# Reordering the opening of a two-layer trunk kernel and spreading its modulation chunks

## The chip, the cores and the metric

The kernel runs on one core of a Trainium2 chip. The metric is device time in microseconds for one whole execution; the median of the runs counts. The core has a matrix engine (PE, with its weight loads shown apart as PEld), a vector engine (DVE), a scalar engine (ACT), a general engine (POOL) and a sequencer (SP) that in this kernel issues every DMA. Each engine works through its own instructions in a fixed order. SP's order matters in the same way: a DMA that must wait for a buffer holds up every DMA behind it.

## The reference

The reference is a backbone of two layers over 1024 latent tokens and 256 context tokens of width 1024. Each layer has two halves, each begun by an RMS norm and a modulation, whose shift, scale and gate come from one product of a small vector with `w_ada`:

```python
def modulation(cond, w_ada, b_ada):
    m = jax.nn.silu(cond) @ w_ada + b_ada
    return [t[..., None, :] for t in jnp.split(m, 6, axis=-1)]
...
sh1, sc1, g1, sh2, sc2, g2 = modulation(c, w_ada[i], b_ada[i])
csh1, csc1, cg1, csh2, csc2, cg2 = modulation(c_ctx, w_ada[i], b_ada[i])
h = modulate(rms_norm(x, norm1_g[i]), sh1, sc1)
hc = modulate(rms_norm(ctx, norm1_g[i]), csh1, csc1)
a_z, bq, bk, bv, cq, ck, cv = split_proj(h @ w_in[i])
...
x = x + g1 * (jnp.concatenate([out_a, out_b, out_c], axis=-1) @ w_out[i])
x = x + g2 * conv_ffn(modulate(rms_norm(x, norm2_g[i]), sh2, sc2), w_up[i], conv_w[i], conv_b[i], w_down[i])
```

The three outputs are a gated MLP over chunks of 128 positions, a windowed attention and a differential attention. All data is float32.

## The kernel before

Tokens are cut into ten tiles of 128: 0 to 7 are latent, 8 and 9 are context. `w_ada` of a layer is [1024, 6144]; the kernel takes its columns in twelve chunks of 512. Chunks 0 and 1 are the shift of the first half, 2 and 3 its scale, 4 and 5 its gate; 6 to 11 are shift, scale and gate of the second half. A chunk is 2 MB, read in four transfers of 512 KB. `mod_chunk` multiplies it on PE with the two vectors, padded to 32 columns, in four 32-column strips of the array at once (line 144), copies the sums out of PSUM (line 146), transposes them (line 149), adds over the strips (line 151) and adds the bias (line 153). `mod_scale` (line 192) then makes the factor of the norm from chunks 2 and 3.

A token tile is loaded and transposed by `load_x` (line 326 is its load, lines 335 to 339 the transposes and copies, line 340 a store of the transposed tile), normalised and modulated by `norm_tile` (lines 208 to 216 the norm, 220 and 222 the modulation, 223 and 109 the split into a high and a low half). The result `h` is what the input projection multiplies.

`inproj` multiplies tiles by one block of 512 columns of `w_in` (blocks 3, 2, 1, 0): 24 matmuls a tile (line 132). The block's weights come in four units of 512 KB (`wunit`, line 113 the load), each split by ACT (line 115) and DVE (line 109) into halves. The raw loads share a ring of three buffers, tag `raw` in pool `wr`; three units of split weights lie in `ws`, the fourth in `wx`. What comes out is copied to a buffer `zs` (line 412, four of them) and goes through norm and rotation (lines 352 to 373), or, in block 0, through the gated MLP (lines 434 to 459), and is stored (lines 391, 463).

Layer 0 takes the tiles in two groups, `al` = (8, 9, 0, 1, 2) and `be` = (3 to 7). In program order: chunks 2, 3, 0, 1; the small tables (`setup`, `setup2`); norms of `al`; blocks 3, 2 of `al`; norms of `be`; blocks 1, 0 of `al` with the context attention; blocks 3, 2, 1 of `be`; chunks 4 to 7; block 0 of `be`; chunks 8 to 11. For chunks 4 to 11 the transfers use the same `raw` ring as the weights. Attention of the latent tiles and the output projection (line 130 with `oT`) follow.

The order on each engine is not the program's. A planner simulates the program and issues, on each engine, what it thinks is ready, earlier code first; so a change in one place moves instructions on all engines for a long way.

Of the kernel before, what the change touches and what calls it, by code (L numbers as in the profile page):

```python
# [52 lines left out]
def trunk(ctx: ExitStack, tc: tile.TileContext, a: dict):  # L53
# [35 lines left out]
    wb = {"zs": 4, "sq": 3, "kn": 3, "st": 2}  # L89
# [45 lines left out]
    def mod_chunk(L, ch, mkps, mkpt, ev, mkraw):  # L135
        ps = mkps()
        for c in range(2):
            for kth in range(2):
                raw = mkraw()
                c0 = ch * 512 + c * 256  # L140
                sp.dma_start(out=raw, in_=a["w_ada"][L, kth * 512:kth * 512 + 512, c0:c0 + 256]
                             .rearrange("(k p) c -> p k c", p=P))
                for j in range(4):
                    pe.matmul(ps[32 * j:32 * j + 32, c * 256:c * 256 + 256], cpad[:, 4 * kth + j, :], raw[:, j, :],
                              start=(kth == 0), stop=(kth == 1))
        dve.tensor_copy(ev, ps)
        pt = mkpt()
# [48 lines left out]
    def norm_tile(L, which, src, s, hi, lo, mkps, mkbig, f=None, ss=None, eng=pool, add='a'):  # L196
# [19 lines left out]
        dve.tensor_tensor(out=f, in0=src, in1=bc[:, 0:P].unsqueeze(1).to_broadcast([P, KT, P]), op=ALU.mult)  # L216
        for k in range(KT):
# [51 lines left out]
    def setup2(ini, L, mkp):  # L269
# [6 lines left out]
        for nm, d in (("c", 32), ("b", 64)):  # L276
            base = ini.tile([P, 2, NT // P, d], F32, tag=f"base{nm}", name="tbase")
            sp.dma_start(out=base, in_=a[f"k_rope_{nm}"].rearrange("(i p) c d -> p c i d", p=P))
            for w in "kq":
# [12 lines left out]
                for c in range(2):  # L292
# [928 lines left out]
```

## Time and profile before

| what | value |
|---|---|
| median of 3 runs | 3370.29 us (3367.59 to 3371.93) |
| the profiled execution | 3366.29 us, its span 3364.5 us |
| PE busy | 3160.1 us, 94% of the span |
| DVE, ACT busy | 2473.2 us (74%), 1669.9 us (50%) |
| mean granted PE clock | 0.971 |
| DMA | 499.50 MB, mean 148 GB/s |

The window view gives, for a stretch of time, busy microseconds of PE, PEld, DVE, ACT and POOL (instruction counts in brackets), the granted PE clock, the busy share of the 16 DMA engines and GB/s. The timeline gives start, duration, engine, line, operation, output and inputs, and in square brackets the idle time before it and what ended it. SPq rows are DMA issues, not transfers. The group view gives busy time and mean nanoseconds of one, and after the bar the idle time before, with what ended it. The matrix engine is busy nearly throughout, so what can be gained there is idle time and time at a reduced clock.

### The profile page before, as it was taken

How to read it: one execution, taken by the hardware profiler on the slowest of the kernel's cores; microseconds unless marked ns; L12 is line 12 of the kernel's file. 1: busy time of each engine (PE TensorE's matmuls, PEld its weight loads, DVE VectorE, ACT ScalarE, POOL GpSimd, SP SyncE). 2: the span in 40 equal slices, each digit the busy share in tenths (PEclk: the TensorE clock that was granted, in tenths of full speed). 3: DMA queues.
4: the chain of work that ended last, by engine and by line, in shares of the span. 5: the costliest groups of instructions: out<-in, count | busy, mean ns of one | idle time of the engine just before them, and what ended most of it. 6: DMA issues, size and time to landing. Idle time of an engine off the chain costs nothing. (4 is left out here: it accounts for less than half of the span.)

```text
span 3364.5 us, 54283 instructions
## 1 busy us (share of the span) xinstructions
PE 3160.1 (94%) x19695; PEld 2760.8 (82%) x19695; DVE 2473.2 (74%) x5666; ACT 1669.9 (50%) x2931; POOL 368.0 (11%) x386
## 2 busy tenths in 40 slices
PE   6999988899998999999999899999999999999999
PEld 4777656787897898998999777767887789999998
DVE  4776765776888895879866578758887686676666
ACT  3555545655555443634334345557565564444443
POOL 0444200100000000100001144101000000000000
PEclk7999988899999999999999999999999999999999
DMA  9555795344442583377433555445555446334433
GB/s 270 172 157 156 222 272 149 100 117 131 126 125 78 169 250 111 103 206 210 131 93 110 161 146 159 126 142 142 155 149 148 114 124 194 112 113 135 132 115 111
DMA packets 766411, 499.50 MB, mean 148 GB/s; under 512 B 81480, under 2 KB 722368, under 8 KB 766144
## 3 DMA queue, kind: packets, MB, share of 16 engines
q1 hardware_dynamic: 766144, 496.03, 51.7%
q8 instruction: 156, 2.56, 0.3%
q14 instruction: 111, 0.91, 0.1%
HBM read 432.48 MB, written 63.44 MB: 147 GB/s over the span
## 5 line engine op out<-in xcount | busy, mean ns | idle before, releaser
L130 PE MATMUL z<-h,wsp 128*128 128x386 f32 (+3 forms) x5280 | 871.5, 318 | 12.5 <-DVE t L844 6.9
L130 PEld LDWEIGHTS z<-h,wsp 128*128 128x128 f32 x5280 | 819.4, 189 | 27.3 <-issue 9.6
L115 ACT ACTIVATE wsp<-raw 128x1024 fp32r<-128x1024 f32 (+2 forms) x660 | 555.8, 846 | 462.1 <-PE z L130 229.8
L109 DVE TENSOR_TENSOR wsp<-raw,wsp 128x1024 fp32r<-128x1024 f32 (+2 forms) x660 | 641.6, 974 | 86.6 <-ACT wsp L115 83.4
L130 PE MATMUL z<-g,wsp 128*128 128x386 f32 (+3 forms) x2640 | 459.9, 322 | 23.3 <-DVE xg L869 9.9
L130 PEld LDWEIGHTS z<-g,wsp 128*128 128x128 f32 x2640 | 416.5, 191 | 40.8 <-issue 13.2
L132 PE MATMUL z<-wsp,h 128*128 128x512 f32 x1584 | 408.3, 404 | 15.5 <-ACT wsp L115 7.3
L132 PEld LDWEIGHTS z<-wsp,h 128*128 128x128 f32 x1584 | 293.1, 192 | 84.7 <-ACT wsp L115 8.2
L130 PE MATMUL zS<-h,wsp 128*128 128x386 f32 (+1 forms) x2112 | 334.8, 314 | 8.0 <-DVE t L844 6.4
L130 PEld LDWEIGHTS zS<-h,wsp 128*128 128x128 f32 x2112 | 319.5, 191 | 10.6 <-issue 6.6
L837 ACT ACTIVATE t<-z,cw 128x386 f32<-128x386 f32 (+3 forms) x220 | 138.3, 629 | 247.2 <-PE z L130 243.8
L841 DVE SCALAR_TENSOR_TENSOR t<-z,cw,t 128x255 f32<-128x255 f32 (+3 forms) x264 | 132.7, 503 | 121.4 <-ACT t L837 120.8
L672 ACT ACTIVATE ec<-ec,nmc 128x1280 f32<-128x1280 f32 (+1 forms) x144 | 182.2, 1266 | 67.3 <-DVE ec L473 66.4
L130 PE MATMUL z<-oT,wsp 128*128 128x384 f32 (+2 forms) x1056 | 199.3, 336 | 3.1 <-DMA oT<-o_s 2.1
L473 DVE TENSOR_SCALAR_CACHE_REDUCE ec<-S,nmc 128x512 f32<-128x512 f32 (+1 forms) x256 | 156.8, 612 | 54.3 <-PE S L669 51.6
L130 PE MATMUL zS<-g,wsp 128*128 128x386 f32 (+1 forms) x1056 | 182.9, 317 | 12.0 <-DVE t L844 4.0
L130 PEld LDWEIGHTS z<-oT,wsp 128*128 128x128 f32 x1056 | 176.7, 189 | 12.0 <-DMA oT<-o_s 2.9
L669 PE MATMUL S<-Kc,qc 128*128 128x512 f32 (+1 forms) x400 | 158.7, 418 | 27.0 <-DVE ec L473 24.3
L869 DVE SCALAR_TENSOR_TENSOR xg<-z,mods,xg 128x384 f32<-128x384 f32 (+5 forms) x288 | 140.4, 501 | 58.0 <-PE z L130 57.8
L130 PEld LDWEIGHTS zS<-g,wsp 128*128 128x128 f32 x1056 | 162.7, 192 | 17.6 <-ACT wsp L115 4.6
L360 POOL TENSOR_TENSOR rs<-ss,cst 128x8 f32<-128x8 f32 (+1 forms) x76 | 116.2, 1529 | 366.6 <-DVE ss L358 293.3
L590 ACT ACTIVATE PT<-T 128x512 f32<-128x512 f32 (+1 forms) x168 | 94.7, 573 | 117.8 <-PE T L586 104.9
(245 smaller groups left out, 4450.5 us busy)
## 6 DMA issues: line engine op xcount, KB each, us to landing
raw<-in_w_up_dram SPq DMA_DIRECT2D x264, 512.0 KB
mraw<-in_w_ada_dram SPq DMA_DIRECT2D x96, 512.0 KB
raw<-in_w_down_dram SPq DMA_DIRECT2D x192, 256.0 KB
Kc<-qk_s SPq DMA_DIRECT2D x96, 320.0 KB
raw<-in_w_in_dram SPq DMA_DIRECT2D x52, 512.0 KB
raw<-in_w_out_dram SPq DMA_DIRECT2D x48, 512.0 KB
raw<-in_w_down_dram SPq DMA_DIRECT2D x104, 192.0 KB
qk_s<-st SPq DMA_DIRECT2D x18, 512.0 KB
```

The source lines that it names most:

```text
L109: eng.tensor_tensor(out=lo, in0=src, in1=hi.bitcast(F32), op=ALU.subtract)
L115: act.activation(out=hl[:, 0], in_=raw, func=AF.Copy)
L130: pe.matmul(ps, w(i, k), h(j, k), start=s, stop=e)
L132: pe.matmul(ps, h(i, k), w(j, k), start=s, stop=e)
L360: pool.tensor_tensor(out=rs[:, :ns], in0=ss[:, 1, :ns], in1=mhalf[:, :ns], op=ALU.pow)
L473: dve.tensor_scalar(out=neg, in0=s_ap, scalar1=-1.0, scalar2=init, op0=ALU.mult, op1=ALU.min, accum_out=acc)
L590: act.activation(out=PT[:, :w_], in_=tp[:, :w_], func=AF.Copy)
L669: pe.matmul(S[:, :w_], q[:, m, ti * P:ti * P + P], K[m][:, o:o + w_], start=True, stop=True)
L672: act.activation(out=e[:, :nk], in_=e[:, :nk], func=AF.Exp, scale=-1.0, bias=acc, accum_out=l1[:, m, ti:ti + 1])
L837: act.activation(out=t[:, o:o + n], in_=ps[:, :n], func=AF.Identity, scale=cw[:, L, 1, ft:ft + 1], bias=cw[:, L, 3, ft:ft + 1])
L841: dve.scalar_tensor_tensor(out=t[:, o + b + 1:o + e], in0=ps[:, b:e - 1], scalar=cw[:, L, 0, ft:ft + 1], in1=t[:, o + b + 1:o + e], op0=AL ...
L869: dve.scalar_tensor_tensor(out=xs, in0=ps[:, b + o0:b + o1], scalar=mods[:, L, 40 + ct, s:s + 1], in1=xs, op0=ALU.mult, op1=ALU.add)
```

## The change

Modulation products are cut differently: `mod_products` reads four transfers of 256 rows by 512 columns instead of 512 rows by 256 columns, and issues per transfer two matmuls of 512 columns in two of the four strips instead of four of 256 columns in all four. The transposes and sums are a function of their own, `mod_finish`, called later. `norm_tile` is split into `norm_front` (the norm, which needs no modulation) and `norm_back`. The last part of `setup2`, the convolution's coefficients, becomes `setup3`.

In the opening, `setup` comes directly after chunk 2, the norms' fronts of tiles 8 and 9 ahead of chunks 3, 0, 1, and that of tile 0 and the weights of block 3 (`w3`) ahead of `setup2`. Chunks 4 to 11 are no longer in two groups of four: 4 stands ahead of block 1 of `al`, 5 ahead of block 0 of `al`, 6 and 7 ahead of blocks 3 and 2 of `be`, 8 and 9 ahead of block 1, 10 and 11 ahead of block 0 of `be`. The `zs` ring has three buffers instead of four.

```diff
-    wb = {"zs": 4, "sq": 3, "kn": 3, "st": 2}
+    wb = {"zs": 3, "sq": 3, "kn": 3, "st": 2}
...
-    def mod_chunk(L, ch, mkps, mkpt, ev, mkraw):
+    def mod_products(L, ch, mkps, ev, mkraw):
         ps = mkps()
-        for c in range(2):
-            for kth in range(2):
-                raw = mkraw()
-                c0 = ch * 512 + c * 256
-                sp.dma_start(out=raw, in_=a["w_ada"][L, kth * 512:kth * 512 + 512, c0:c0 + 256]
-                             .rearrange("(k p) c -> p k c", p=P))
-                for j in range(4):
-                    pe.matmul(ps[32 * j:32 * j + 32, c * 256:c * 256 + 256], cpad[:, 4 * kth + j, :], raw[:, j, :],
-                              start=(kth == 0), stop=(kth == 1))
+        for q in range(4):
+            raw = mkraw()
+            sp.dma_start(out=raw, in_=a["w_ada"][L, q * 256:q * 256 + 256, ch * 512:ch * 512 + 512]
+                         .rearrange("(k p) c -> p k c", p=P))
+            for i in range(2):
+                j = 2 * (q % 2) + i
+                pe.matmul(ps[32 * j:32 * j + 32, :], cpad[:, 2 * q + i, :], raw[:, i, :], start=(q < 2), stop=(q >= 2))
         dve.tensor_copy(ev, ps)
+
+    def mod_finish(L, ch, mkpt, ev):
         pt = mkpt()
...
-    modset(0, (2,), ini, "mev", ini, "mraw", 16, mkz, mkU)
-    pre = [load_x(i, nwk, mkT) for i in (8, 9)]
-    modset(0, (3, 0, 1), ini, "mev", ini, "mraw", 16, mkz, mkU)
+    modset(0, (2,), ini, ini, "mraw", 16)()
     setup(ini, mkU)
+
+    def load_norm(i):
+        xc, ss = load_x(i, nwk, mkT)
+        norm_front(xc, mkT, None, xc, ss)
+        return xc, "done"
+
+    pre = [load_norm(i) for i in (8, 9)]
+    for ch in (3, 0, 1):
+        modset(0, (ch,), ini, ini, "mraw", 16)()
     mod_scale(0, 0)
+    w3 = inproj_w(0, 3, wx)
+    pre.append(load_norm(0))
     ini.release()
...
-    ipset(0, al, (3, 2))
+    ipset(0, al, (3, 2), w=w3)
+    setup3(ini2, 0, mkU)
...
+    later = lambda ch: modset(0, (ch,), wk, wr, "raw", 3)
+
+    m = later(4)
     ipset(0, al, (1,))
+    m()
...
+    m = later(5)
     ipset(0, al, (0,))
+    m()
     st["wd"] = 1
-    ipset(0, be, (3, 2))
+    for ch, cb in ((6, 3), (7, 2)):
+        m = later(ch)
+        ipset(0, be, (cb,))
+        m()
     for hd in range(4):
         attn_c(0, hd, [(0, 1)], at, mkS, mkT, mkO)
-    ipset(0, be, (1,))
-    modset(0, range(4, 8), wk, "kn", wr, "raw", 3, mkz, mkU)
-    ipset(0, be, (0,))
-    modset(0, range(8, 12), wk, "kn", wr, "raw", 3, mkz, mkU)
+    for ch, cb in (((8, 9), 1), ((10, 11), 0)):
+        for c in ch:
+            m = later(c)
+            if c == ch[0]:
+                m()
+        ipset(0, be, (cb,))
+        m()
     mod_scale(0, 1)
```

Three places on the engines, as the planner orders them. `mraw` is a transfer of `w_ada`, `raw` a unit of `w_in`, `xin` a token tile, `x_s` its store, `tbase`, `gt`, `tb`, `tab_ck` the rotation tables, `cr` the convolution's coefficients.

SP in the opening, before, from just behind the last transfer of chunk 1 and the small rows of `setup` to the first weights:

```order
L326 DMA xin<-in_x_dram 128x1024 x2
L272 DMA mk<-in_k_mask_dram 128x384
L278 DMA tbase<-in_k_rope_c_dram 128x20x32
L281 DMA gt<-in_c_knorm_dram 128x32
L281 DMA gt<-in_c_qnorm_dram 128x32
L278 DMA tbase<-in_k_rope_b_dram 128x20x64
L298 DMA snk<-in_b_sink_dram 128x8
L301 DMA lp<-in_c_lam_dram 128x128
L312 DMA cr<-in_conv_w_dram 44x128 x3
L313 DMA cr<-in_conv_b_dram 44x128
L113 DMA raw<-in_w_in_dram 128x2x512 x3
```

The same place now, from the last two transfers of chunk 1:

```order
L139 DMA mraw<-in_w_ada_dram 128x2x512 x2
L113 DMA raw<-in_w_in_dram 128x2x512 x3
L335 DMA xin<-in_x_dram 128x1024 x2
L279 DMA mk<-in_k_mask_dram 128x384
L349 DMA x_s<-xc 1024x1x128
L285 DMA tbase<-in_k_rope_c_dram 128x20x32
```

Three units of block 3 now go ahead of the tables. The fourth unit (first of the next three `raw`) stands behind them, where before it stood behind the first table stores as well:

```order
L308 DMA lp<-in_c_lam_dram 128x128
L321 DMA cr<-in_conv_w_dram 44x128 x3
L322 DMA cr<-in_conv_b_dram 44x128
L113 DMA raw<-in_w_in_dram 128x2x512 x3
L300 DMA tab_ck_98<-tb 128x10x32 x2
L288 DMA gt<-in_b_knorm_dram 128x64
```

PE in the opening, before, from the transposes of chunk 1 on:

```order
L149 MATMUL U<-cst,mev 128x128 x4
L257 MATMUL U<-cst,rows 128x42
L335 MATMUL T<-cst,xin 128x128 x8
L214 MATMUL T<-dg,cst 128x128
L335 MATMUL T<-cst,xin 128x128 x8
L316 MATMUL U<-cst,cr 128x44 x4
L214 MATMUL T<-dg,cst 128x128
L132 MATMUL z<-wsp,h 128x512 x7
```

And now:

```order
L149 MATMUL U<-cst,mev 128x128 x4
L344 MATMUL T<-cst,xin 128x128 x4
L132 MATMUL z<-wsp,h 128x512 x13
L344 MATMUL T<-cst,xin 128x128 x4
L132 MATMUL z<-wsp,h 128x512 x5
L214 MATMUL T<-dg,cst 128x128
```

Between the modulation and the first projection matmul there is now half a transposed token tile, where there were two whole tiles, two norm broadcasts and the coefficients.

PE between blocks 1 and 0 of `al`, before (no modulation here):

```order
L132 MATMUL z<-wsp,h 128x512 x19
L265 MATMUL U<-cst,wsr 128x128 x4
L132 MATMUL z<-wsp,h 128x512 x23
L379 MATMUL U<-cst,kn 128x128 x4
L132 MATMUL z<-wsp,h 128x512 x26
```

The same place now, with chunk 5 in it:

```order
L272 MATMUL U<-cst,wsr 128x128 x4
L132 MATMUL z<-wsp,h 128x512 x2
L143 MATMUL z<-mraw,cpad 32x512 x6
L388 MATMUL U<-cst,kn 128x128 x4
L143 MATMUL z<-mraw,cpad 32x512 x2
L388 MATMUL U<-cst,kn 128x128 x8
L132 MATMUL z<-wsp,h 128x512 x18
```

Chunk 5's eight matmuls now stand between the last matmul of one block and the first of the next. The SP rows that feed this place now:

```order
L139 DMA mraw<-in_w_ada_dram 128x2x512 x2
L361 DMA tab<-tab_cq_100 128x2x32
L361 DMA tab<-tab_bq_101 128x128 x2
L400 DMA qk_s_87<-st 128x6x128
L361 DMA tab<-tab_bq_101 128x128
L400 DMA qk_s_87<-st 128x6x128
L361 DMA tab<-tab_bq_101 128x128 x2
L139 DMA mraw<-in_w_ada_dram 128x2x512
L113 DMA raw<-in_w_in_dram 128x2x512 x3
```

The first three transfers of the chunk hold all three `raw` buffers; the fourth and the next block's weights follow behind them in the ring.

More of the change, by code (lines that the diff above doesn't have):

```diff
@@ L193, in mod_scale, with norm_front @@
                                      in1=g, op0=ALU.add, op1=ALU.mult)
-    def norm_tile(L, which, src, s, hi, lo, mkps, mkbig, f=None, ss=None, eng=pool, add='a'):
+    def norm_front(src, mkps, mkbig, f=None, ss=None):
         ms = sm.tile([P, 2], F32, tag="nms", name="nms")
@@ L216, in norm_tile, with norm_back @@
         dve.tensor_tensor(out=f, in0=src, in1=bc[:, 0:P].unsqueeze(1).to_broadcast([P, KT, P]), op=ALU.mult)
+        return f
+    def norm_back(L, which, f, s, hi, lo, eng=pool, add='a'):
         for k in range(KT):
@@ L224, in norm_tile @@
         sub(eng, lo, f, hi)
+    def norm_tile(L, which, src, s, hi, lo, mkps, mkbig, f=None, ss=None, eng=pool, add='a'):
+        norm_back(L, which, norm_front(src, mkps, mkbig, f, ss), s, hi, lo, eng, add)
     def setup_c(ini, ips):
@@ L309, in setup2, with setup3 @@
                                  op0=ALU.add, op1=ALU.subtract)
+    def setup3(ini, L, mkp):
         cr = ini.tile([2 * NFF, 4, P], F32, tag="cr", name="cr")
@@ L968, in norms @@
         q = pre or [load(i) for i in tiles[:ahead]]
-        ahead = max(ahead, len(q))
+        ahead = 2 if pre else ahead
         for n, i in enumerate(tiles):
-            q += [load(j) for j in tiles[n + ahead:n + ahead + 1]]
+            q += [load(j) for j in tiles[len(q):n + ahead + 1]]
             xc, ss = q[n]
             h = hp.tile([P, 2, KT, P], F32R, tag="h", name="h")
-            norm_tile(L, 0, xc, int(i >= NLT), h[:, 0], h[:, 1], mk, big, xc, ss, E_[eng[n % len(eng)]], add[n % len(add)])
+            if ss != "done":
+                norm_front(xc, mk, big, xc, ss)
+            norm_back(L, 0, xc, int(i >= NLT), h[:, 0], h[:, 1], E_[eng[n % len(eng)]], add[n % len(add)])
             hts[i] = h
@@ L979, in trunk @@
     ini2 = mkpool("ini2", 1, "left")
+    wx = mkpool("wx0", 1, "right")
     ini = mkpool("ini", 1, "right")
@@ L1000, in trunk @@
     wk = mkpool("wk0", 2, "right")
-    wx = mkpool("wx0", 1, "right")
     hts = {}
@@ L1096, in hook @@
             setup2(ini, 1, mkT)
+            setup3(ini, 1, mkT)
         if f == NH[0]:
```

14 lines of the change are left out of this document (10 added, 4 removed).

## The prediction

> **What bounds the kernel now.** I read the page first, then the windows of the first 600 us, then the timeline where a window has a hole. The page says that the matrix engine is the bound almost everywhere:
>
> ```profile
> span 3364.5 us, 54283 instructions
> PE 3160.1 (94%) x19695; PEld 2760.8 (82%) x19695; DVE 2473.2 (74%) x5666; ACT 1669.9 (50%) x2931; POOL 368.0 (11%) x386
> ```
>
> So 204 us of the span are PE idle, and the change can only touch what lies in its first 600 us. The windows there (busy PE, PEld, DVE, ACT, POOL, then granted clock, DMA share, GB/s) show two holes and a dense stretch between:
>
> ```profile
> 20.00:40.00 20.00, 10.54 (x87) 3.93 (x88) 3.80 (x15) 0.38 (x1) 0.00 (x0) 0.69 0.93 294
> 36.00:60.00 24.00, 13.25 (x47) 9.62 (x48) 15.89 (x43) 13.04 (x23) 1.81 (x3) 0.54 0.92 252
> 60.00:92.00 32.00, 28.22 (x124) 22.59 (x123) 22.12 (x50) 18.84 (x35) 8.83 (x10) 0.95 0.84 222
> 84.00:168.00 84.00, 79.36 (x365) 64.22 (x363) 61.88 (x141) 42.61 (x79) 41.24 (x50) 0.96 0.57 172
> 252.00:336.00 84.00, 83.67 (x480) 61.95 (x478) 57.69 (x209) 42.28 (x103) 37.60 (x46) 1.00 0.54 156
> 400.00:420.00 20.00, 20.00 (x132) 15.05 (x130) 13.54 (x43) 10.87 (x22) 4.42 (x5) 1.00 0.17 45
> 420.00:440.00 20.00, 15.42 (x93) 9.29 (x85) 12.61 (x45) 7.49 (x15) 2.69 (x3) 0.67 0.96 263
> 440.00:460.00 20.00, 16.62 (x148) 9.21 (x147) 13.79 (x48) 8.05 (x18) 1.93 (x1) 0.99 0.90 269
> 460.00:480.00 20.00, 15.82 (x93) 12.46 (x94) 10.71 (x26) 8.95 (x14) 0.00 (x0) 0.74 0.96 280
> 480.00:500.00 20.00, 17.14 (x114) 12.99 (x113) 10.88 (x46) 9.05 (x20) 0.70 (x1) 0.91 0.95 281
> 500.00:520.00 20.00, 13.52 (x78) 9.39 (x79) 7.35 (x36) 8.44 (x19) 0.74 (x1) 0.83 0.54 155
> ```
>
> The first hole is the opening: DMA over 0.9, PE half busy at a clock of 0.54 to 0.69. From 84 to 336 us PE is 91 to 100% busy while DMA stands at 0.54 to 0.57, so it has room. The second hole is 420 to 520: five windows, 21.5 us of PE idle, DMA at 0.90 to 0.96 in four of them. Busy time times what is missing of the clock adds 5.1 + 0.2 + 4.1 + 1.5 + 2.3 = 13.2 us. Just before, DMA is nearly idle (0.17), and the queue view says why, with the group view saying who paid:
>
> ```profile
> SPq L463 <- ACT st L382: 19.6, 2, 19.2
> L144 PE MATMUL z<-mraw,cpad 128*32 128x256 f32 x128 | 12.0, 436 | 7.2 <-DMA mraw<-in_w_ada_dram 7.2
> L144 PE MATMUL z<-mraw,cpad 128*32 128x256 f32 x128 | 10.8, 389 | 1.9 <-DMA mraw<-in_w_ada_dram 1.9
> L545 PE MATMUL S<-Kb,qb 128*128 128x384 f32 x10 | 4.6, 461 | 5.6 <-DMA qb<-qk_s 4.6 <-DVE pb L473 1.0
> L130 PE MATMUL z<-oT,wsp 128*128 128x384 f32 x48 | 10.2, 352 | 1.9 <-DMA oT<-o_s 1.9
> ```
>
> (The second row is of 400 to 520 us, the third of 320 to 400.) SP stood 19.2 us at a store of the gated MLP, with transfers of chunks 8 to 11 queued behind it. Then everything arrives at once, and PE waits 7.2 us for modulation and 6.5 us for attention and projection operands that share the DMA engines.
>
> **The opening: -10.** The rows that set it:
>
> ```profile
> 32.50 1.08 PE L144 MATMUL z<-mraw,cpad 128*32 128x256 f32 x8 [0.35 <-DMA mraw<-in_w_ada_dram]
> 35.77 0.17 DVE L153 TENSOR_TENSOR mods<-mods,bcol 128x8 f32<-128x8 f32 x1
> 36.01 0.44 SPq L272 DMA_DIRECT2D mk<-in_k_mask_dram  x1
> 43.77 1.65 ACT L222 ACTIVATE xc<-xc,mods,amod 128x128 f32<-128x128 f32 x4 [1.34 <-DVE xc L216]
> 46.19 1.06 ACT L223 ACTIVATE h<-xc 128x1024 fp32r<-128x1024 f32 x1 [0.77 <-ACT xc L222]
> 47.63 1.41 SPq L113 DMA_DIRECT2D raw<-in_w_in_dram  x3
> 52.73 0.80 PE L132 MATMUL z<-wsp,h 128*128 128x512 f32 x1 [2.58 <-ACT wsp L115]
> 67.52 1.06 ACT L115 ACTIVATE wsp<-raw 128x1024 fp32r<-128x1024 f32 x1 [6.16 <-DMA raw<-in_w_in_dram]
> 80.83 1.22 DVE L109 TENSOR_TENSOR h<-xc,h 128x1024 fp32r<-128x1024 f32 x1
> 81.94 10.36 PE L132 MATMUL z<-wsp,h 128*128 128x512 f32 x44
> GB/s 328 310 369 376 389 384 415 420 399 410 379 366 364 348 346 351 348 351 341 356 346 346 346 356 340 356 348 348 338 356 343 353 346 351 343 356 348 348 340 387
> ```
>
> The last transfer of chunk 1 landed at 32.5. The last row is the DMA rate from 8 to 24 us: about 348 GB/s in modulation transfers, 1.5 us per 512 KB. One tile store now stands ahead of it, so it lands at 34.0. From landing to the last sum took 35.9 - 32.5 = 3.4 us: 37.4. The norm's front is done, so tile 8 needs only its modulation (1.65) and the split (1.06): 40.1. Three weight units land behind chunk 1 at 35.5, 37.0 and 38.5; PE's next row is half a token tile, which lands one place later, at 40.0. So the first projection matmul starts at about 41 instead of 52.7, 12 us earlier.
>
> That lead shrinks. The fourth unit stands behind eleven table entries, which took SP from 36.0 to 47.6; counted from 33 it is issued near 46 and there by 50, against 67.5. But h of the fifth tile is DVE work: 15.9 + 22.1 = 38 us of it lie between 36 and 92. Begun at 35 and 78% busy, it ends near 84, where the first block ended at 81.94 + 10.36 = 92.3. Lead 8 us. I take -10, between the two; bounds -4 (half the lead lost to table work in the same DVE queue) and -16 (the fourth unit's lead kept whole).
>
> The transfers now move rows of 2 KB instead of 1 KB. In the rate row the stretch with 4 KB token rows reached 399 to 420, so 8.4 MB could take 20.2 to 24.1 us; the sum takes none of that, the lower bound above holds it. [...]
>
> **The second hole: -19.** Chunks 4 to 7 are consumed before the blocks of `be`, 8 to 11 inside them, in time that had DMA at about 0.55. Direct waits that go: 7.2 + 1.9 = 9.1. Of the 6.5 us for attention and projection operands I take half, 3.3, since those queues are re-ordered too; of the 13.2 us of clock half, 6.6. Bounds: -9 (the direct waits alone) and -36 (all idle, all clock).
>
> **The handovers: +9.** Chunks sit between blocks and share the ring of three with the weights. After the second raw pair frees a buffer, the next block's first unit must be fetched and split while PE has only what the order shows: two raw pairs and twelve transposes for chunk 5. The price of fetch and split, and of the cover:
>
> ```profile
> 91.09 0.38 SPq L113 DMA_DIRECT2D raw<-in_w_in_dram  x1
> 94.80 1.06 ACT L115 ACTIVATE wsp<-raw 128x1024 fp32r<-128x1024 f32 x1 [1.19 <-DMA raw<-in_w_in_dram]
> 91.75 1.22 DVE L109 TENSOR_TENSOR wsp<-raw,wsp 128x1024 fp32r<-128x1024 f32 x1
> 173.49 0.60 PE L379 MATMUL U<-cst,kn 128*128 128x128 f32 x4
> 425.38 0.64 PE L144 MATMUL z<-mraw,cpad 128*32 128x256 f32 x8 [2.23 <-DMA mraw<-in_w_ada_dram]
> ```
>
> Fetch 94.8 - 91.1 = 3.7, plus 1.06, plus 1.22: 6.0 us. Cover: two raws at 0.64 and three times 0.6 for transposes, 3.1. That leaves a hole of about 3 us at chunk 5 and as much at chunk 4. At the other four places attention rows stand between; I take 0.75 each. Sum 9; bounds 0 (all covered) and 36 (6.0 at all six). Queued behind the waiting matmul is the whole next block, as PE goes in order.
>
> A hole also costs clock: in 420 to 440 the clock was 0.67, though the longest single wait that PE had there was 2.23 us. [...]
>
> **The products themselves: +5.** Before, four strips ran side by side; now two per transfer.
>
> ```profile
> L144 PE MATMUL z<-mraw,cpad 128*32 128x256 f32 x384 | 36.2, 446 | 18.0 <-DMA mraw<-in_w_ada_dram 18.0
> L596 PE MATMUL O<-PT,Vb 128*64 128x256 f32 x184 | 31.8, 405 | 0.1
> ```
>
> Four strips: 36.2/384 = 0.094 us a record of 256 columns, 3.0 a chunk. The nearest row with only two groups side by side is L596: 31.8/184 = 0.173. A chunk now has 16 records of 512 columns: 3.0 us if neighbouring transfers overlap, 5.5 if not. For the eight late chunks 0 to +20; I take +5, as the first transfers of a chunk lie ready and the last ones wait anyway. In the opening the DMA covers it.
>
> The smaller `zs` ring, `setup3` and the moved `setup` I cost at nothing. For the ring the row is that of the layer's whole input projection:
>
> ```profile
> L132 PE MATMUL z<-wsp,h 128*128 128x512 f32 x960 | 247.2, 407 | 12.9 <-ACT wsp L115 7.3 <-DVE wsp L109 3.1 <-ACT zs L412 2.4
> ```
>
> PE waited 2.4 us for the copy into `zs`, and what empties the ring, ACT and POOL, is half free there. If that cover is gone, one tile less of lead (24 x 0.26 = 6.2 us) is missing in each pass of block 0, 12 us; the range holds it.
>
> Sum: -10 - 19 + 9 + 5 = -15 on the profiled execution's 3366.3, so 3351. The median was 4.0 above that execution; the same offset gives 3355, and I say **3354**.
>
> **Rivals.** (B) *The handovers are covered and the second hole closes*: attention matmuls fill, the hole yields 28 instead of 19, opening 12: 3370 - 28 - 12 + 3 = 3333. For it: 0.17 DMA share before the jam shows that the bandwidth was there. Against: chunks 4 and 5 have no attention beside them in the order. (C) *A wait takes the place of the one removed*: the ring of three serialises chunk and weights at all six places at 6.0 us, and the clock falls after them. 36 + 6 - 10 - 19 = +13: 3383. For it: the fourth transfer and the next units are behind the chunk's own release in SP's order. Against: the four late places have attention rows. It decides from (10 + 19 - 5)/6 = 4.0 us a place. (D) *It doesn't reach the end*: the planner re-orders all that follows, SP meets another store like that of L463, and the second hole re-forms around attention loads; opening 6, direct waits 9, handovers and products 14: 3370 - 1 = 3369. For it: only 9.1 of the 21.5 us idle is modulation.
>
> **How the numbers follow.** Forecast 0.46 (own range 3342 to 3363), B 0.18, C 0.20, D 0.16. A measurement here tells about 0.2% from no change, 6.7 us, so the limits are 3363.6 and 3377.0. Faster takes the forecast and B, 0.64; no change D, 0.16; slower C, 0.20. The range runs from below B, 3330, to C's near half, 3380.
>
> **What would show it.** Right: the first projection matmul near 41 us and the first block's end near 84; DMA share between 84 and 336 above 0.62 and that of 420 to 500 below 0.8; no wait on `mraw` over 3 us; holes of 2 to 4 us before the first matmul of blocks 1 and 0 of `al`. Wrong: a start of the projection later than 47, a PE window after 420 still at 15 of 20, waits on weight units (ACT split behind a `w_in` transfer) of more than 4 us at several handovers, or a product record of 512 columns costing over 0.3 us.

## The result: 1.0% slower

| | before | changed |
|---|---|---|
| median | 3371.11 us (3367.59 to 3372.16, 4 runs) | 3402.77 us (3401.17 to 3409.43, 4 runs) |
| profiled execution, its span | 3366.29, 3364.5 us | 3401.17, 3399.4 us |
| ratio | | 1.010, 95% interval 1.0082 to 1.0117 |

The forecast was 3354, with a range of 3330 to 3380. The page of the changed kernel begins:

```profile
span 3399.4 us, 53886 instructions
PE 3189.6 (94%) x19503; PEld 2772.6 (82%) x19503; DVE 2478.5 (73%) x5666; ACT 1671.0 (49%) x2931; POOL 362.8 (11%) x386
```

Of the 34.9 us that the span grew, 29.5 are busy time of PE and 5.4 are idle time. So most of the loss does not show as waiting. The windows of the changed kernel, cut as the prediction cut those of before:

```profile
20.00:40.00 20.00, 13.85 (x66) 3.72 (x58) 6.22 (x15) 2.99 (x4) 0.00 (x0) 0.84 1.05 390
...
60.00:92.00 32.00, 25.54 (x105) 19.93 (x106) 23.71 (x58) 17.96 (x36) 11.58 (x14) 0.79 0.87 230
84.00:168.00 84.00, 76.96 (x349) 59.05 (x348) 61.50 (x143) 39.93 (x77) 43.30 (x52) 0.92 0.66 194
252.00:336.00 84.00, 80.71 (x420) 57.91 (x419) 54.26 (x206) 38.59 (x100) 32.30 (x44) 0.98 0.56 156
...
420.00:440.00 20.00, 17.66 (x97) 10.33 (x96) 12.99 (x40) 9.12 (x16) 0.00 (x0) 0.84 0.99 293
440.00:460.00 20.00, 19.18 (x98) 14.97 (x98) 14.40 (x33) 13.13 (x21) 2.04 (x4) 0.97 0.66 191
460.00:480.00 20.00, 20.00 (x108) 15.46 (x106) 14.96 (x41) 11.32 (x20) 4.85 (x4) 1.00 0.26 73
480.00:500.00 20.00, 15.46 (x103) 12.19 (x102) 16.94 (x57) 10.85 (x22) 5.25 (x5) 0.83 0.84 263
500.00:520.00 20.00, 16.87 (x86) 13.49 (x87) 8.77 (x41) 7.29 (x18) 0.70 (x1) 0.74 0.76 228
```

At the same hours the second hole has shrunk: 21.5 us of PE idle in 420 to 520 have become 10.8 (by the work done it has moved more than it has closed, as the experiments will show). But the dense stretch is no longer dense: 84 to 168 fell from 79.36 to 76.96 busy and from 0.96 to 0.92 in clock, 252 to 336 from 83.67 to 80.71 and from 1.00 to 0.98.

Windows at the same hour hold different work, so I also followed the work. From the matmul records of two traces I counted the columns streamed, four times for float32, without the modulation products. "Behind at t" is the time at which a kernel has done what the kernel before had done at t, minus t. This table is worked out, not a view of the profile; the kernels below the first row are the experiments. Each row compares one profiled execution with that of the kernel before, which is 5 us below its median; the others lie within 4 us of theirs, but that of e8 is 9 above.

| behind the kernel before (us) at | 120 | 200 | 320 | 520 | 1000 | 1300 | 3300 |
|---|---|---|---|---|---|---|---|
| changed kernel | 0 | 30 | 54 | 25 | 28 | 36 | 35 |
| e1 opening, cut, three zs, no spread | -1 | 8 | 4 | -11 | -10 | -2 | 4 |
| e2 spread, three zs | 0 | 29 | 50 | 21 | 25 | 33 | 36 |
| e3 changed, old cut | -2 | 24 | 45 | 18 | 18 | 18 | 17 |
| e5 three zs | 1 | 17 | 7 | 6 | 6 | 7 | 8 |
| e6 changed, no transfers | 1 | 18 | 29 | -8 | -8 | -6 | -11 |
| e7 changed, weights first | 0 | 33 | 61 | 33 | 38 | 48 | 52 |
| e8 opening, three zs | -2 | 16 | 6 | 3 | 9 | 20 | 5 |
| e9 changed, pairs in `be` | 0 | 19 | 49 | 1 | 1 | 8 | 1 |
| e10 changed, later loads | 0 | 30 | 54 | 23 | 22 | 26 | 28 |
| e11 opening, cut, later loads | 1 | -4 | -5 | -18 | -15 | -15 | -7 |
| e12 cut | 4 | -1 | 1 | -3 | 5 | 15 | -2 |
| e13 opening | -1 | -2 | -2 | -10 | -15 | -15 | -13 |
| e14 changed, own buffer | 1 | 57 | 86 | 83 | 107 | 105 | 111 |
| e15 changed, only 4 and 5 spread | 1 | 20 | 11 | 12 | 17 | 24 | 29 |
| e16 pairs, four zs, later loads | 0 | 23 | 42 | 0 | -2 | -1 | 0 |

(At 200 and 320 a spread kernel has paid for products that the grouped ones pay after 324 us; 520 is the first fair place.) The changed kernel loses 25 us by 520 us, 3 more by 1000, 8 between 1000 and 1300, and nothing after.

**By 520 us.** The same work, from what the kernel before did at 100 us to what it did at 520, split by what PE did in it (again worked out from the records; the last column is the part of the other busy time that went by a granted clock below 1, from the clock records of the traces):

| us | length | PE idle | only products on PE | other PE busy | of it lost to the clock |
|---|---|---|---|---|---|
| before | 420 | 37 | 21 | 362 | 18 |
| changed | 446 | 46 | 27 | 373 | 27 |
| e1 (no spread) | 410 | 26 | 33 | 352 | 8 |
| e6 (no transfers) | 412 | 34 | 18 | 361 | 16 |
| e7 (weights first) | 453 | 52 | 34 | 368 | 23 |
| e14 (own buffer) | 502 | 56 | 74 | 373 | 21 |

Over the whole stretch the other matmuls are nearly the same in all rows, so a longer "other busy" is mostly lower clock. The loss of 26 is 9 idle, 6 products and 11 other busy, 9 of it by the granted clock. The groups of 100 to 520 us say where PE waited, first of the kernel before, then of the changed one:

```profile
L132 PE MATMUL z<-wsp,h 128*128 128x512 f32 x814 | 207.8, 405 | 6.1 <-DVE wsp L109 2.6 <-ACT wsp L115 1.9 <-ACT zs L412 1.6
L144 PE MATMUL z<-mraw,cpad 128*32 128x256 f32 x256 | 22.8, 413 | 9.1 <-DMA mraw<-in_w_ada_dram 9.1
```

```profile
L132 PE MATMUL z<-wsp,h 128*128 128x512 f32 x811 | 216.7, 414 | 15.5 <-ACT wsp L115 9.2 <-DVE wsp L109 4.2 <-ACT zs L421 1.2
L143 PE MATMUL z<-mraw,cpad 128*32 128x512 f32 x128 | 28.6, 632 | 9.9 <-DMA mraw<-in_w_ada_dram 9.9
```

The projection (L132) waits 8.9 us more for split weights (9.2 + 4.2 against 1.9 + 2.6) and is busy 8.9 us longer at nearly the same count. The products still wait 9.9 us for their transfers: spreading has not removed that wait, it has moved it. The timeline of PE at the handovers of chunks 4 and 5 in the changed kernel:

```profile
131.34 1.92 PE L143 MATMUL z<-mraw,cpad 128*32 128x512 f32 x4 [3.95 <-DMA mraw<-in_w_ada_dram]
136.06 1.22 PE L132 MATMUL z<-wsp,h 128*128 128x512 f32 x2 [2.39 <-ACT wsp L115]
138.27 1.22 PE L132 MATMUL z<-wsp,h 128*128 128x512 f32 x2 [0.51 <-DVE wsp L109]
...
175.39 1.92 PE L143 MATMUL z<-mraw,cpad 128*32 128x512 f32 x4 [2.73 <-DMA mraw<-in_w_ada_dram]
179.77 0.66 PE L388 MATMUL U<-cst,kn 128*128 128x128 f32 x4 [1.41 <-DVE st L109]
181.50 0.95 PE L132 MATMUL z<-wsp,h 128*128 128x512 f32 x2 [0.85 <-DVE wsp L109]
...
283.40 1.05 PE L143 MATMUL z<-mraw,cpad 128*32 128x512 f32 x4 [1.20 <-DMA mraw<-in_w_ada_dram]
```

Each of these two handovers has two holes in a row. The first is for the chunk's last transfer (3.95 and 2.73 us), which I had not counted. The second is, at chunk 4, the wait for the weights that I had counted (2.39 us); at chunk 5 it is 1.41 us for `st` and 0.85 us for weights. The four records of two products (each is two records) take 1.92 us there; in the last row, chunk 7 after a hole of 1.20 us, four records take 1.05.

**Near 1190 us.** The issues of SP and the split of ACT in the changed kernel, and PE's wait:

```profile
1192.88 1.23 SPq L761 DMA_DIRECT2D o_s<-stc  x2
1194.16 0.59 SPq L785 DMA_DIRECT2D oT<-o_s  x1
...
1195.43 3.35 SPq L785 DMA_DIRECT2D oT<-o_s  x6
1198.87 0.61 SPq L113 DMA_DIRECT2D raw<-in_w_down_dram  x1
...
1210.03 0.63 ACT L115 ACTIVATE wsp<-raw 128x512 fp32r<-128x512 f32 x1 [12.30 <-DMA raw<-in_w_down_dram]
1210.71 4.32 PE L130 MATMUL zS<-g,wsp 128*128 128x386 f32 x12 [5.23 <-ACT wsp L115]
```

A weight unit of `w_down` is queued behind seven operand loads of the next output projection; ACT then waits 12.3 us for a unit, and PE 5.2 us for ACT. In the kernel before those loads stand behind a run of `w_up` units that were asked for ahead of them:

```profile
1184.12 9.70 SPq L113 DMA_DIRECT2D raw<-in_w_up_dram  x4
...
1197.88 1.24 SPq L752 DMA_DIRECT2D o_s<-stc  x2
1199.16 1.69 SPq L776 DMA_DIRECT2D oT<-o_s  x3
...
1203.41 3.02 SPq L776 DMA_DIRECT2D oT<-o_s  x4
```

Nothing of the diff touches this place; the planner's order came out otherwise there.

### The profile page after: what moved, and what is told of

It reads as the page before. It is cut to its first block, busy times and chain, and to the rows that moved or that the text cites. A ratio compares the mean times of both kernels' runs of the same rounds, so it can differ in the third digit from the quotient of the medians.

```text
span 3399.4 us, 53886 instructions
## 1 busy us (share of the span) xinstructions
PE 3189.6 (94%) x19503; PEld 2772.6 (82%) x19503; DVE 2478.5 (73%) x5666; ACT 1671.0 (49%) x2931; POOL 362.8 (11%) x386
## 5 line engine op out<-in xcount | busy, mean ns | idle before, releaser
L130 PE MATMUL z<-g,wsp 128*128 128x386 f32 (+3 forms) x2640 | 461.7, 323 | 24.7 <-DVE t L853 9.4
L132 PE MATMUL z<-wsp,h 128*128 128x512 f32 x1584 | 421.2, 411 | 22.4 <-ACT wsp L115 9.2
L132 PEld LDWEIGHTS z<-wsp,h 128*128 128x128 f32 x1584 | 297.7, 196 | 94.9 <-ACT wsp L115 11.0
L130 PEld LDWEIGHTS z<-oT,wsp 128*128 128x128 f32 x1056 | 178.6, 190 | 14.4 <-issue 5.0
```

Source lines behind the costliest of these rows:

```text
L130: pe.matmul(ps, w(i, k), h(j, k), start=s, stop=e)
L132: pe.matmul(ps, h(i, k), w(j, k), start=s, stop=e)
```

## The experiments

Each is compared with runs of the kernel before on the same chip.

| run | median us | ratio, 95% interval |
|---|---|---|
| e1 | 3367.8 | 0.9995 (0.9983 to 1.0008) |
| e2 | 3401.7 | 1.0095 (1.0079 to 1.0111) |
| e3 | 3384.8 | 1.0044 (1.0029 to 1.0059) |
| e5 | 3374.5 | 1.0017 (1.0008 to 1.0027) |
| e6 | 3352.9 | 0.9952 (0.9937 to 0.9967) |
| e7 | 3416.0 | 1.0136 (1.0121 to 1.0152) |
| e8 | 3362.7 | 0.9979 (0.9969 to 0.9988) |
| e9 | 3369.1 | 1.0003 (0.9993 to 1.0014) |
| e10 | 3395.0 | 1.0078 (1.0059 to 1.0098) |
| e11 | 3354.9 | 0.9950 (0.9936 to 0.9965) |
| e12 | 3360.6 | 0.9967 (0.9956 to 0.9979) |
| e13 | 3356.7 | 0.9957 (0.9941 to 0.9972) |
| e14 | 3477.0 | 1.0324 (1.0310 to 1.0338) |
| e15 | 3394.0 | 1.0078 (1.0063 to 1.0094) |
| e16 | 3364.8 | 0.9993 (0.9985 to 1.0002) |

### Is it the spread? (e1, e2)

e1 puts the chunks back into groups:

```diff
-    m = later(4)
     ipset(0, al, (1,))
-    m()
...
     ipset(0, be, (1,))
+    for ch in range(4, 8):
+        later(ch)()
     ipset(0, be, (0,))
+    for ch in range(8, 12):
+        later(ch)()
```

> The changed kernel with chunks 4 to 11 put back into two groups of four (4 to 7 ahead of block 0 of be, 8 to 11 behind it); the new opening, the new cut of the products and three zs buffers stay. Theory H (the loss is made at the handovers, where a chunk's transfers stand ahead of the next block's weights in the shared ring): the kernel is back near 3371, plus about 3 us for the new cut: 3371 to 3377, and by 520 us it is less than 8 us behind the kernel before instead of 25. Theory O (the new opening costs, or shifts everything behind it): 3390 or more, since the opening is all there. Theory F (the two-strip products cost it): about 3377. Theory L (12 us of the loss are a late w_down load near 1190 us, an accident of the planner's order): that load may be late or not here; if H is right and it is late too, 3384.

e2 is the kernel before with the places of the change, the old cut and three `zs` buffers:

```diff
-    wb = {"zs": 4, "sq": 3, "kn": 3, "st": 2}
+    wb = {"zs": 3, "sq": 3, "kn": 3, "st": 2}
...
+    m = mod_later(4)
     ipset(0, al, (1,))
+    m()
```

> The kernel before with nothing but chunks 4 to 11 spread as in the change (old opening, old four-strip products, and three zs buffers, since the chunk's own sum buffer needs the room). Theory H: the loss is here too, 18 to 25 us by 520 us: 3389 to 3396, or about 3403 if the late load near 1190 us comes with it. Theory O: the loss is gone, 3368 to 3375. Theory F: gone as well, since the old cut is back.

Without the spread the loss is gone: 3367.8, no difference from before. With the spread, without the new opening and cut, all of it is there: 3401.7 (of which three `zs` buffers alone cost some 6 us by 520 us, see e5). So it is the spread. e1 was 11 us ahead at 520 us and lost most of that near 1190 us.

### The cut of the products (e3)

```diff
-        for q in range(4):
+        for c in range(2):
+            for kth in range(2):
```

> The changed kernel with the products cut as before (four transfers of 512 rows by 256 columns, four strips at once). Theory F: the group of products was 28.6 us in the changed kernel against 22.8 before between 100 and 520 us, so 6 us come back, and up to 10 more if the two-strip form also lowers the clock: 3386 to 3396. Theory H and theory O: no more than those 6 us, 3396 to 3402.

18 us came back, more than the 6 of the products. The table splits it: 7 by 520 us and 11 behind it, where its order has the loads near 1190 us as the kernel before has them (it stays 17 to 18 behind from 520 to the end). That is a result on the order, not on the cut.

### Weights ahead of the chunk (e7)

```diff
+    w = inproj_w(0, 1, wx)
     m = later(4)
-    ipset(0, al, (1,))
+    ipset(0, al, (1,), w=w)
```

> The changed kernel with the four weight units of a block asked for ahead of the chunk that stands at its handover, so that the chunk's transfers are queued behind the block's weights instead of ahead of them, and its products fall inside the block. Theory H: the waits of the projection on split weights (15.5 and 9.2 us between 100 and 520 us in the changed kernel, in all 18 us above those of before) go back to 6 to 10 us, and with them most of the lost clock: 3378 to 3388. Theories O and F: 3398 to 3404, as neither the opening nor the products change. Theory L: the load near 1190 us may come out late or not; if not, 12 us less on either side.

My theory at that point, that the order of chunk and weights in the ring was the trouble, fell: 3416, slower still. The groups of 100 to 520 us show the exchange:

```profile
L132 PE MATMUL z<-wsp,h 128*128 128x512 f32 x812 | 212.4, 410 | 3.6 <-ACT zs L421 2.8 <-DVE mev L144 0.8
L143 PE MATMUL z<-mraw,cpad 128*32 128x512 f32 x128 | 35.2, 666 | 14.4 <-DMA mraw<-in_w_ada_dram 14.3
```

The wait for weights is wholly gone (15.5 became 3.6, none of it on `wsp`), and the wait for the chunk rose from 9.9 to 14.4. The products now stand inside the block, still ahead of the landing of their transfers, and PE takes them in their turn: at 129.01 us they follow a wait of 2.09 us for `mraw`, and the block's matmuls behind them run from 130.86 us without a wait of their own.

### No transfers (e6)

```diff
-            raw = mkraw()
-            sp.dma_start(out=raw, in_=a["w_ada"][L, q * 256:q * 256 + 256, ch * 512:ch * 512 + 512]
-                         .rearrange("(k p) c -> p k c", p=P))
+            raw = cpad.rearrange("p k c -> p (k c)").unsqueeze(1).to_broadcast([P, 2, 256])
```

(For chunks 4 to 11 only.)

> The changed kernel without the transfers of chunks 4 to 11: their products multiply a block that lies in the buffer memory already, so the matmuls, their places and their sums stay, and the 16 MB of w_ada and their turns in the ring of three go (the modulation of the layer's gates and of its second half is therefore not the reference's). Theory T (the spread costs because its transfers stand in the ring and in the DMA queues: waits for them, for the weights behind them, and the clock that the waits cost): by 520 us the kernel is level with the kernel before or up to 15 us ahead, instead of 25 behind; 3355 to 3372, or 12 more if the late w_down load near 1190 us stays. Theory P (the products themselves, cut into the projection, cost it): it stays 15 us or more behind by 520 us, 3385 to 3400.

3352.9, and 8 us ahead at 520 us. The groups:

```profile
L132 PE MATMUL z<-wsp,h 128*128 128x512 f32 x815 | 208.9, 405 | 8.5 <-ACT zs L424 7.3 <-DVE wsp L109 0.8 <-ACT wsp L115 0.3
L146 PE MATMUL z<-cpad 128*32 128x512 f32 x128 | 18.3, 599 | 0.0
```

All three parts of the loss go with the transfers: idle 46 to 34, products 27 to 18, other busy 373 to 361. The products at the same places cost little (18.3 us busy and no wait, against 28.6 and 9.9); what costs is that PE meets them before their data. The kernel before has the same 16 MB to move, so this is no way to save time, only to see the cause. That run has no late load near 1190 us either.

### Which handovers (e9, e15)

```diff
-    for ch, cb in ((6, 3), (7, 2)):
+    for ch, cb in (((4, 5), 3), ((6, 7), 2), ((8, 9), 1), ((10, 11), 0)):
```

> The changed kernel with two chunks ahead of each of the four blocks of be (4 and 5, 6 and 7, 8 and 9, 10 and 11) and none at the two blocks of al. Theory of places (each handover costs once, whatever number of chunks it takes, and the two of al cost about 15 us each, those of be 4 to 10): 15 to 25 us of the loss by 520 us go, 0 to 10 us behind there; 3371 to 3381, or 12 more with the late load near 1190 us. Theory of chunks (each chunk costs its transfers wherever it stands): still some 20 us behind by 520 us, 3390 to 3402.

```diff
     m = later(5)
     ipset(0, al, (0,))
     m()
...
+    for ch in (6, 7):
+        later(ch)()
     ipset(0, be, (0,))
+    for ch in range(8, 12):
+        later(ch)()
```

> The counterpart of the run with pairs: only chunks 4 and 5 are spread (ahead of blocks 1 and 0 of al, as in the change), 6 and 7 stay together ahead of block 0 of be and 8 to 11 behind it; the rest as in the changed kernel. If the two handovers of al are where the loss is: about 30 us behind at 200 us as in the changed kernel, and 10 to 25 behind at 520 us, since two chunks less stand in the later hole: 3382 to 3396. If every handover costs alike: a third of the loss, 5 to 10 us behind at 520 us, 3374 to 3382.

At 520 us: e1 (none) -11, e15 (only the two of `al`) 12, e9 (only the four of `be`, with two chunks more) 1, changed kernel (all six) 25. By these totals the two handovers of `al` cost 23 us (e15 against e1) or 24 (changed kernel against e9), the four of `be` 13 or 12. I had priced them at 3 and 0.75 us each. e9 came 2 us below its range for places; e15 is inside its range, but was 20 behind at 200 us, not 30.

The totals don't say where the time goes. The split by the work does, in two halves: ahead of the slash the work that the kernel before did from 100 to 330 us, behind it that from 330 to 520 us.

| us | PE idle | lost to the clock | only products on PE |
|---|---|---|---|
| before | 12 / 25 | 6 / 12 | 2 / 19 |
| changed | 27 / 19 | 12 / 15 | 21 / 6 |
| e1 (none) | 17 / 9 | 5 / 3 | 0 / 33 |
| e15 (two of `al`) | 17 / 24 | 5 / 11 | 10 / 20 |
| e9 (four of `be`) | 22 / 8 | 7 / 5 | 25 / 7 |

The windows of these two halves, of e1 and of e15:

```profile
98.62:331.03 232.41, 215.84 (x1084) 169.17 (x1083) 171.87 (x514) 119.32 (x268) 106.97 (x120) 0.97 0.54 155
331.03:508.90 177.87, 168.93 (x967) 102.30 (x967) 114.25 (x374) 90.20 (x172) 17.97 (x21) 0.96 0.81 239
```

```profile
100.36:343.65 243.29, 226.44 (x1123) 171.21 (x1121) 172.41 (x506) 117.88 (x260) 100.92 (x119) 0.96 0.59 173
343.65:531.60 187.95, 164.15 (x925) 105.46 (x925) 114.85 (x378) 92.72 (x182) 20.18 (x22) 0.91 0.72 206
```

In the first half e15, which has both handovers of `al`, idles no longer than e1, which has none, and loses no more clock; it is 11 us behind there by products that e1 pays later. Its 15 us of idle time and 8 of clock above e1 lie in the second half: the second hole closes in e1 and in e9 and stays open in e15 and in the changed kernel. In that hole PE of the changed kernel waits for a load of the attention (320 to 540 us) about as long as before, 4.6 us; e1 and e9 have no such wait:

```profile
PE S L554 <- DMA qb<-qk_s: 4.8, 1, 4.8
```

So chunks at `al` do cost some 23 us by 520 us, but not as a hole at each place, and no price per handover follows. Why the hole stays open with them is not shown; the planner has re-ordered that stretch in each run.

### The smaller `zs` ring (e5)

```diff
-    wb = {"zs": 4, "sq": 3, "kn": 3, "st": 2}
+    wb = {"zs": 3, "sq": 3, "kn": 3, "st": 2}
```

> The kernel before with three zs buffers instead of four and nothing else. If the smaller ring costs, as the bound of the prediction had it, 6 to 12 us: 3376 to 3383. If it is free: 3366 to 3374. A difference that starts far from the projection (the load near 1190 us) would show that any small edit re-plans that place.

Small but not free: 3374.5, between my two ranges and 0.17% slower, behind from 140 us on, where the projection fills the ring, and 6 us behind at 520 us.

### The late load (e10)

```diff
-HK = (16, 13, 20, 12)
+HK = (18, 13, 20, 12)
```

> The changed kernel with one number changed far from the change: the operands of the second token group's output projection are asked for two blocks of the first MLP later (18 instead of 16). In the order this puts those sixteen loads of o_s and x_s among the w_up units; in the changed kernel they stand among the last w_down units near 1190 us, where ACT waited 12.3 us for one of these. Theory L (that wait is 12 to 15 us of the loss and comes from the loads beside it, not from the chunks): level with the changed kernel to about 1000 us, then 10 to 15 us ahead of it: 3387 to 3393. If the place costs the same whatever stands there: 3398 to 3404.

The waits of ACT for weights between 1100 and 1270 us (total, times, longest), in the kernel before, the changed one and e10:

```profile
ACT wsp L115 <- DMA raw<-in_w_down_dram: 8.8, 6, 3.7
```

```profile
ACT wsp L115 <- DMA raw<-in_w_down_dram: 16.5, 4, 12.3
```

```profile
ACT wsp L115 <- DMA raw<-in_w_down_dram: 3.6, 1, 3.6
```

The long wait is gone, and by the work e10 is 26 behind at 1300 us instead of 36. But it was not level with the changed kernel before: at 1000 us it is 22 behind instead of 28. From 1000 to 1300 us e10 loses 4 where the changed kernel loses 8. So about 4 of the 10 us go with the late load, and 6 come from an order that differs ahead of it. The median shows 8 in all (3395.0 against 3402.8, and the intervals of the two ratios overlap).

### The opening and the cut by themselves (e8, e12, e13)

e8 is e1 with the old cut; e13 is e8 with four `zs` buffers; e12 is the kernel before with the new cut.

```diff
-            ev = evp.tile([P, 512], F32, tag="mev", name="mev", bufs=1)
+            evt = "kn" if rawp is wr else "mev"
+            ev = evp.tile([P, 512], F32, tag=evt, name="mev", bufs=wb.get(evt, 1))
```

(The edit from e8 to e13, beside `"zs": 4`: the sums go into the old ring `kn`, which makes the room.)

> The new opening and three zs buffers with the chunks in the two old groups and the old four-strip products. With the new cut this kernel was 11 us ahead of the kernel before at 520 us and lost 13 to 18 at the late w_down load near 1190 us. If that lead is the opening's and the order's, it is here too: 8 to 14 us ahead at 520 us; if it is the new cut's, level with before there. If the late load is an accident of the order, it may be missing: then 3357 to 3362 in the first case; with it 3368 to 3374.

> The new opening alone: old cut, chunks in the two old groups, four zs buffers. With three zs buffers it was 3 us behind the kernel before at 520 us; three buffers alone were 6 us behind. So the opening should be worth 0 to 4 us: 3 us ahead at 520 us. Its order has the loads near 1190 us where the kernel before has them: no loss there, 3364 to 3370. If my prediction's 10 us for the opening were there: 3357 to 3361.

> The kernel before with the products cut as in the change (two strips at once, rows of 2 KB) and nothing else. By the product rows the cut costs 0.6 to 0.9 us a chunk, 5 to 7 us for the eight late chunks, if PE is the limit there; where the transfers are (the two groups of four) it costs nothing, and rows of 2 KB may save some. By 520 us: level, within 4 us. It stands in the order with the loads among the w_down units near 1190 us, so 10 to 15 us may go there: 3380; if not, 3366 to 3374.

e8 is 3 behind at 520 us, so the lead that e1 has there is not the opening's and the order's alone; its median, 3362.7, is just above the range that I gave for a lead, which its trace doesn't show. I missed on e13 in the good direction: the new opening alone gives 3356.7, 14 us less than before, and on e12: the new cut alone 3360.6, 10 less. But the trace of e13 is only 1 to 2 us ahead until 320 us; its gain of 10 to 15 falls between 400 and 700 us, where SP's longest wait for `st` at the gated MLP's store is 5.8 us instead of 19.2. e12 is 3 ahead at 520, loses 17 by 1300 us, most of it near 1190 us (ACT's longest wait for `w_down` there is 16.1 us), and has them back by 2600 us. What of these gains is the edit and what is the re-planned order is open; no run separates them.

### Own buffer for the spread chunks (e14)

```diff
+                if own:
+                    rw = mkraw()
+                    r0 = q * 256 + i * P
+                    sp.dma_start(out=rw, in_=a["w_ada"][L, r0:r0 + P, ch * 512:ch * 512 + 512])
...
-    later = lambda ch: modset(0, (ch,), wk, wr, "raw", 3)
+    later = lambda ch: modset(0, (ch,), wk, wk, "mown", 1)
```

> The changed kernel with the spread chunks out of the weights' ring: each of chunks 4 to 11 comes in eight transfers of 256 KB through one buffer of its own, and its sums go into the old ring of three (which makes the room). The order then lays the products singly between tiles of the projection. Theory R (at a handover the chunk and the next block's weights wait for each other in the ring of three): the waits on split weights at the six places go, 0 to 10 us behind the kernel before at 520 us instead of 25, 3370 to 3386. Theory D (16 MB more in the queues and eight waits for a transfer that the order puts too early, whatever the ring): still 15 us or more behind at 520 us, 3388 to 3402.

Worst of all, 3477, outside what either theory gave. The groups of 100 to 520 us:

```profile
L132 PE MATMUL z<-wsp,h 128*128 128x512 f32 x698 | 180.8, 405 | 3.0 <-ACT zs L428 1.7 <-DVE mev L151 1.0
L149 PE MATMUL z<-mraw,cpad 128*32 128x512 f32 x100 | 61.0, 696 | 30.0 <-DMA mraw<-in_w_ada_dram 30.0
```

No wait on split weights is left, now that no chunk stands in their ring. But with one buffer each product waits for its own transfer (30.0 us for 100 records), and where a product stands alone a record costs 0.61 us of PE (61.0/100) against 0.22 in the changed kernel (28.6/128), where up to four products run side by side. A single small buffer is not a fair test of an own ring; a larger one was not tried.

### Versions that are faster than both (e11, e16)

e11 is e1 with four `zs` buffers and e10's later loads. e16 is e9 with the same two edits.

> The parts that the runs so far showed to help or to cost nothing, without the spread: the new opening, the new cut, the chunks in their two old groups, four zs buffers again (the chunk's sums go into the old ring of three), and the later loads of the second token group. With three zs buffers the same arrangement was 11 us ahead of the kernel before at 520 us; the fourth buffer should give up to 6 more, and the load near 1190 us should cost nothing: 3350 to 3358. If the gain by 520 us was an accident of the order, 3365 to 3372.

> Two chunks ahead of each block of be, none at al, with four zs buffers and the later loads of the second token group. With three buffers and the earlier loads the pairs were 1 us behind the kernel before at 520 us. Four buffers should give 6, the loads near 1190 us nothing to lose: 3355 to 3365. The same without any spread had 3354.9: if the pairs close the hole of 420 to 520 us better than the two groups of four, 3345 to 3353.

e11 takes 3354.9, 0.5% less than before, with the chunks in their old groups. e16, the same with pairs spread over `be`, takes 3364.8. So no spread that I tried beats the two groups, even with everything else at its best. The group of products of e1 shows part of why the groups are no longer dear: its 128 records wait 2.6 us, where the 256 of the kernel before waited 9.1.

```profile
L143 PE MATMUL z<-mraw,cpad 128*32 128x512 f32 x128 | 35.0, 647 | 2.6 <-DMA mraw<-in_w_ada_dram 2.6
```

## Why the prediction was wrong, step by step

**The opening: -10.** This step failed: the first steps came nearly as forecast, the end did not. The changed kernel's timeline, rows of DVE, PE and SP:

```profile
40.57 0.16 DVE L153 TENSOR_TENSOR mods<-mods,bcol 128x8 f32<-128x8 f32 x1
...
43.59 1.22 PE L132 MATMUL z<-wsp,h 128*128 128x512 f32 x2 [1.68 <-ACT h L227]
...
58.11 0.37 SPq L335 DMA_DIRECT2D xin<-in_x_dram  x1
58.58 0.55 SPq L349 DMA_DIRECT2D x_s<-xc  x1
...
63.30 1.08 PE L344 MATMUL T<-cst,xin 128*128 128x128 f32 x4 [3.67 <-DMA xin<-in_x_dram]
```

The kernel before:

```profile
49.16 0.40 SPq L326 DMA_DIRECT2D xin<-in_x_dram  x1
49.66 0.55 SPq L340 DMA_DIRECT2D x_s<-xc  x1
```

The sum was there at 40.7, not 37.4, and the projection began at 43.6, not 41. I then let the lead shrink from 12 to 8 us by DVE. The 78% of that sum stands in no row; DVE's two rows give 66 and 69%, with which the lead would have been about 1 us. In the trace it shrank by SP: the load of the block's last tile, and the store of the tile that is third in the block, which its norm waits for until 64.7 us, are issued 9 us later than before. They stand behind the table entries, which I had followed for the weights but not for the tiles. The first block ended at 92.1 us, not near 84, and at 100 us the changed kernel is 1 us ahead. That the opening alone saves 14 us in the end (e13) does not make the step right: those came after 400 us, in another way than I had worked out.

**The second hole: -19.** This step failed too. Over the work that the kernel before did from 330 to 520 us, idle went from 24.7 to 19.0, and the clock took 15.0 instead of 12.1: 3 us gained, under my lower bound of 9. The direct wait for modulation went as I said (the products wait 0.7 us there), but the wait for the attention's load stayed, at 4.8 us. And the spread is not what closes the hole: in e1, without it, idle there is 8.9 and the clock takes 3.1.

**The handovers: +9.** This is the step that failed at the largest cost. Over the work of 100 to 330 us idle rose by 14.6 (12.1 to 26.7) and the time lost to the clock by 6.1 (5.8 to 11.9): 21. (Other busy rose by 18.8 there, but that is not all clock: by then the changed kernel has done 68 matmuls of 128x512 fewer, and more transposes and attention matmuls.) Against e1, which lacks only the spread, the cost by 520 us is 36: 20 idle and 21 other busy, 19 of it clock, less 6 of products. Three things were left out or too small. I priced one hole for the weights and none for the chunk's own last transfer (3.95 and 2.73 us). The 0.75 for each of the four later places stood on no row. And the clock, which I kept out of the sum, is about half of the cost against e1. My bound of 36 held all this; the choice near the lower end did not, and the row that should have decided, 0.67 of clock in 420 to 440 behind a wait of 2.23 us, stood in the prediction.

In the terms of the sum, then: opening -1 instead of -10, second hole -3 instead of -19, handovers +21 instead of +9, products +6 instead of +5, some 10 for what lies behind 520 us, and 2 that I can't place. That is +35 where I had -15.

**The clock behind a hole.** In the changed kernel the granted clock fell in both holes at the chunks' last transfers. Of the 3.95 us ahead of chunk 4 it was 1.00 over the first 3.25 and 0.50 over the last 0.68; of the 2.73 us ahead of chunk 5 it was 1.00 over the first 2.36 and 0.50 over the last 0.35. Behind each, four records of 512 columns took 1.92 us. They took 1.92 us as well behind holes of 2.09 and 2.26 us in e7 (at 129.01 and 230.14 us), but 1.38 behind one of 2.18 us there (at 171.10) and 1.05 behind the 1.20 us at chunk 7 of the changed kernel. In the kernel before, eight records of 256 columns took 0.64 us behind the 2.23 us, and the clock fell only 1.4 us after the hole's end, to 0.50 until 440 us. In e2 eight such records took 0.64 us behind 2.33 us (at 129.39) and 1.08 behind 2.64 (at 171.98). So a hole of 2 to 3 us was followed by half clock in some places here and not in others, and what else it takes is not shown.

**The products: +5.** Right: 28.6 against 22.8 us, 5.8 more.

**The `zs` ring at nothing.** Wrong by 6 us by 520 us (e5), under the bound of 12 that I had given for a lost cover.

**Not in the sum at all:** what lies behind 520 us, some 10 us, 8 of them between 1000 and 1300 us. The late load near 1190 us, in an order re-planned 700 us behind the last edit, is in it; e10 gives back 4 of the 8.

**Rivals.** C (3383, a wait takes the place of the one removed) came nearest, at 0.20. Its point of decision, 4.0 us a place, was passed as a mean by e1 (36/6 = 6.0), though the time does not lie at the places alone. Its mechanism was half right: the ring did make the weights wait, but e7 shows that freeing the weights only moves the wait to the chunk. Even C fell 20 us short, because it kept -10 for the opening and -19 for the second hole, and neither came. D (no change, at 0.16), whose hole re-forms around attention loads, had that in part: the wait of 4.8 us for `qb`. Of the signs I named for being right, "no wait on `mraw` over 3 us" failed at once (3.95), and a DMA share above 0.62 held for 84 to 168 (0.66) and not for 252 to 336 (0.56). One sign of being wrong came: a PE window after 420 us at 15 of 20 (15.46 in 480 to 500).

## What to carry to other kernels

Work that needed its own transfer was not free here, though the DMA engines had room (a share of 0.54 to 0.57 from 84 to 336 us in the kernel before): where it stood ahead of the landing of that transfer PE had a hole (3.95 and 2.73 us at chunks 4 and 5), and the clock fell to 0.50 before either hole ended. So a few dense groups can be cheaper than many thin ones: 3354.9 us for two groups (e11) against 3364.8 for pairs (e16), the rest alike. Don't credit a change with closing a hole that has a second wait in it. Price each place with both waits and with the clock, and test a price near the lower bound against the worst row of the same trace. Where a planner orders the program, compare the order far behind the edit too, go by work done and not by the hour, and split a change into its parts: here the opening and the cut were 0.4 and 0.3% faster alone, part of it perhaps by a luckier order, and the spread hid that.

## What the hardware showed that I had not expected

A product in one 32-column strip took PE nearly as long alone as with three others beside it. In the timelines one product took 1.05 us (e14, at 164.34 us, two records), two side by side 1.05 (changed kernel, at 283.40, four records) and four 1.07 (e7, at 178.64, eight records). Over the groups a record cost 0.61 us where the products stood singly (e14, 61.0/100, some of them at lower clock) and 0.14 where nothing had to be waited for and they stood together (e6, 18.3/128). Laying them singly among full matmuls made each some four times as dear in PE's busy time, the waits apart.
